# Feed-forward layers in two phases through DRAM, with seven block products in place of eight in 21 of 24 up-projection pairs

## The chip, the cores and the metric

The kernel runs on one core of a Trainium2 chip. The metric is the device time of one execution in microseconds (us), as the median of the runs shown. The engines are TensorE (PE in the rows; PEld is its weight load), VectorE (DVE), ScalarE (ACT), GpSimd (POOL) and SyncE (SP), which only issues transfers here.

## What is computed

A decoder of two layers on 1024 tokens with 1024 features, all in float32. Layer 0 mixes tokens with an RG-LRU, layer 1 with stick-breaking attention; behind each stands a gated feed-forward network, which is what the change touches:

```python
D_MODEL = 1024; SEQ = 1024; D_FF = 3 * D_MODEL; FFN_CONV = 3

def causal_depthwise_conv(x, w, b):
    K = w.shape[0]
    S = x.shape[1]
    xp = jnp.pad(x, ((0, 0), (K - 1, 0), (0, 0)))
    y = b + xp[:, 0:S] * w[0]
    for k in range(1, K):
        y = y + xp[:, k:k + S] * w[k]
    return y

def conv_ffn(x, w_up, conv_w, conv_b, w_down):
    h = causal_depthwise_conv(x @ w_up, conv_w, conv_b)
    return (jax.nn.gelu(h[..., :D_FF]) * h[..., D_FF:]) @ w_down

# per layer, with mix the RG-LRU (layer 0) or the attention (layer 1)
x = layer_norm(DN_ALPHA * x + mix, ln_g[layer, 0], ln_b[layer, 0])
f = conv_ffn(x, ffn_w_up[layer], ffn_conv_w[layer], ffn_conv_b[layer], ffn_w_down[layer])
x = layer_norm(DN_ALPHA * x + f, ln_g[layer, 1], ln_b[layer, 1])
```

## The kernel before

Float32 operands are held as a sum of two `fp32r` parts (`Split`: `hi`, a rounded copy, and `lo`, the rest). A product of two such operands is three matmuls: hi by hi, hi by lo, lo by hi. The residual stream `xres` is eight tiles of 128 tokens by 1024 features; its transpose `xT` (features by tokens, in two halves of 512 tokens) is made by `transpose_x`: PE transposes into PSUM, ACT casts the hi part (L219), DVE subtracts the lo part (L220).

Four stages follow each other: RG-LRU, feed-forward of layer 0, attention, feed-forward of layer 1. `ffn(layer, last)` goes over 24 pairs `j` of blocks of 128 hidden features, one gate block (`pg`) and one value block (`pu`). For each block `wblock` issues one load of 512 KB on SP's queue, a cast of the hi part on ACT (L83) and the subtraction of the lo part on POOL (L89). `project` makes 48 matmuls of 128x512 for a block (eight blocks of the contraction, two halves of the tokens, three matmuls each), so 96 for a pair. Pair 0 is done in quarters of 256 tokens (`project_quarter`, `mm3`) while the last tiles of the stage before are still being finished. `conv` does the convolution of width 3 from PSUM: an ACT Identity with scale and bias (L406) and two DVE multiply-adds (L408). Then come the gelu on ACT (L429), the product of gate and value on DVE (L431), and the split of the gated values on POOL (`mh` L87, `ml` L89), which stay in SBUF.

After every second pair `accumulate` adds the product of two earlier gated blocks and two blocks of `w_down` to `xres`: for each of eight token tiles 12 matmuls (L137, L138, L141) and two DVE additions (L149). The last four blocks go through `Finish`, tile by tile: the rest of the sum, the statistics on DVE (L162, L164), `rstd` on POOL (L166, L167), the normalisation (DVE L189, then ACT L192 and POOL L193, or DVE L196 for the last tiles), and what follows a tile: its transposes, or the store of the output.

The order on each engine is fixed when the program is built, by a scheduler that works from the tile pools (number of buffers per tag) and the order of the calls. An engine runs its instructions in that order; a wait at the head holds what stands behind it. All loads of weights stand in SP's queue in the same way.

## Time and profile before

| | before |
|---|---|
| median of 3 runs | 2514.78 us (2513.81 to 2517.9) |
| span of the profiled execution | 2509.8 us |
| PE busy | 2427.3 us, 97% of the span |
| DVE, POOL, ACT busy | 47%, 38%, 28% of the span |
| transfers | 125.71 MB, 50 GB/s over the span |
| first pair after the quarters, layer 0 and layer 1 | 369.2 us and 1733.8 us |
| last matmul of layer 0's and of layer 1's feed-forward | about 1139 us and 2496 us |

The profiled execution has no time of its own beside its span; the span is 5.0 us under the median of the runs. A busy engine in such a table is busy by the modelled ends of its instructions. A row of a timeline gives the start, the duration, the engine, the line, the operation with output and inputs, and in brackets how long the engine sat idle before it and what released it. A row of the groups by line gives count, sum and mean.

### The profile page before, as it was taken

The page shows a single profiled execution, that of the slowest core. Times are in us where ns is not written, and L with a number is a line of the kernel's source. Part 1 is how long each engine was busy: PE and PEld are TensorE (multiplying, and loading weights), DVE is VectorE, ACT ScalarE, POOL GpSimd, SP SyncE. Part 2 cuts the span into 40 slices and gives each one's busy share as a digit, 9 for nine tenths or more (in the row PEclk, how much of TensorE's full clock was granted, in tenths as well). Part 3 has the DMA queues.
Part 4 walks back from the last instruction along what each step waited for, and adds up shares of the span by engine and source line. Part 5 has one row for each costly group of instructions (what it writes and reads, how often), then busy time and mean ns, then how long its engine had stood idle before and what let it go on. Part 6 is the DMA issues. An engine that isn't in the chain of part 4 may idle for free.

```text
span 2509.8 us, 27143 instructions
## 1 busy us (share of the span) xinstructions
PE 2427.3 (97%) x11324; PEld 2008.6 (80%) x11324; DVE 1182.8 (47%) x1400; ACT 713.3 (28%) x951; POOL 953.0 (38%) x570
## 2 busy tenths in 40 slices
PE   8999889999999999999999999989999999999997
PEld 6877778888888888878877787768888888888886
DVE  5684852333333333364466555594433333333336
ACT  4644232212111122223433333343222122121221
POOL 4685354333333323353322222254533323333334
PEclk9999999999999999999999999999999999999999
DMA  6111112111111111210011101111211111111112
GB/s 216 47 53 51 42 34 60 50 51 51 46 47 51 51 50 43 68 42 26 28 32 34 29 31 34 35 33 43 76 43 51 48 45 51 45 48 51 51 34 84
DMA packets 36410, 125.71 MB, mean 50 GB/s; under 512 B 4032, under 2 KB 5696, under 8 KB 36288
## 3 DMA queue, kind: packets, MB, share of 16 engines
q1 hardware_dynamic: 31680, 110.11, 14.1%
q10 hardware_dynamic: 4608, 13.87, 1.7%
q8 instruction: 89, 1.46, 0.2%
q14 instruction: 33, 0.27, 0.0%
HBM read 119.78 MB, written 4.19 MB: 49 GB/s over the span
## 4 chain that ended last, share of the span: by engine, by line
PE 41%; DVE 5%; issue 5%; POOL 1%; ACT 1%; POOLq 0%; DVEq 0%; ACTq 0%
PE po L137 3%; PE pg L111 3%; PE pu L111 3%; PE pg L114 3%; PE pu L112 3%; PE pg L112 3%; PE po L141 3%; PE po L138 3%; PE pu L114 3%; PE pp L101 2%; PE pp L103 2%; PE pp L102 2%; DVE e L578 2%; DVE xres L549 1%; DVE b L579 1%
## 5 line engine op out<-in xcount | busy, mean ns | idle before, releaser
L89 POOL TENSOR_TENSOR wlo<-wraw,whi 128x1024 fp32r<-128x1024 f32 (+2 forms) x213 | 519.3, 2440 | 1082.8 <-ACT whi L83 1068.6
L83 ACT CAST whi<-wraw 128x1024 fp32r<-128x1024 f32 (+2 forms) x205 | 206.9, 1010 | 1139.5 <-PE pg L112 341.1
L137 PE MATMUL po<-whi,mh 128*128 128x512 f32 x896 | 353.1, 395 | 14.1 <-DVE xres L149 12.7
L138 PE MATMUL po<-wlo,mh 128*128 128x512 f32 x896 | 351.5, 392 | 0.0
L408 DVE SCALAR_TENSOR_TENSOR u<-pg,pv,u 128x1023 f32<-128x1023 f32 x96 | 123.1, 1282 | 436.9 <-ACT u L406 435.2
L149 DVE TENSOR_TENSOR xres<-xres,po 128x512 f32<-128x512 f32 x390 | 252.0, 681 | 162.6 <-PE po L141 160.3
L408 DVE SCALAR_TENSOR_TENSOR u<-pu,pv,u 128x1023 f32<-128x1023 f32 x96 | 123.0, 1281 | 392.3 <-ACT u L406 391.3
L112 PE MATMUL pg<-xTl,whi 128*128 128x512 f32 x736 | 286.3, 389 | 0.0
L111 PE MATMUL pg<-xTh,whi 128*128 128x512 f32 x736 | 286.3, 389 | 0.0
L111 PE MATMUL pu<-xTh,whi 128*128 128x512 f32 x736 | 286.3, 389 | 0.0
L112 PE MATMUL pu<-xTl,whi 128*128 128x512 f32 x736 | 286.3, 389 | 0.0
L141 PE MATMUL po<-whi,ml 128*128 128x512 f32 x896 | 280.6, 392 | 0.0
L114 PE MATMUL pg<-xTh,wlo 128*128 128x512 f32 x736 | 226.6, 389 | 0.0
L114 PE MATMUL pu<-xTh,wlo 128*128 128x512 f32 x736 | 226.6, 389 | 0.0
L137 PEld LDWEIGHTS po<-whi,mh 128*128 128x128 f32 x896 | 169.5, 189 | 56.6 <-DVE xres L149 16.4
L141 PEld LDWEIGHTS po<-whi,ml 128*128 128x128 f32 x896 | 169.3, 189 | 36.3
L138 PEld LDWEIGHTS po<-wlo,mh 128*128 128x128 f32 x896 | 169.7, 189 | 34.7
L101 PE MATMUL pp<-xTh,whi 128*128 128x512 f32 (+1 forms) x416 | 161.3, 388 | 0.0
L114 PEld LDWEIGHTS pg<-xTh,wlo 128*128 128x128 f32 x736 | 138.2, 188 | 28.7
L114 PEld LDWEIGHTS pu<-xTh,wlo 128*128 128x128 f32 x736 | 138.2, 188 | 28.7
L112 PEld LDWEIGHTS pu<-xTl,whi 128*128 128x128 f32 x736 | 138.2, 188 | 28.7
L111 PEld LDWEIGHTS pu<-xTh,whi 128*128 128x128 f32 x736 | 138.2, 188 | 28.6
(166 smaller groups left out, 3968.4 us busy)
## 6 DMA issues: line engine op xcount, KB each, us to landing
wraw<-in_w_up SPq DMA_DIRECT2D x96, 512.0 KB, 3.5
wraw<-in_w_down SPq DMA_DIRECT2D x48, 512.0 KB, 3.5
wraw<-in_w_in SPq DMA_DIRECT2D x14, 512.0 KB, 3.6
wraw<-in_w_o SPq DMA_DIRECT2D x9, 512.0 KB, 3.5
xres<-in_x ACTq DMA_DIRECT2D x8, 512.0 KB, 4.9
wraw<-in_w_out SPq DMA_DIRECT2D x8, 512.0 KB, 3.5
wraw<-in_w_q SPq DMA_DIRECT2D x8, 512.0 KB, 3.5
wraw<-in_w_k SPq DMA_DIRECT2D x8, 512.0 KB, 3.5
```

What stands on the lines that cost most here:

```text
L83: A.copy(out=hi, in_=src)
L89: eng.tensor_tensor(out=lo, in0=src, in1=hi.bitcast(F32), op=ALU.subtract)
L101: T.matmul(out, lhsT=l.hi, rhs=r.hi, start=start, stop=False)
L102: T.matmul(out, lhsT=l.hi, rhs=r.lo, start=False, stop=False)
L111: T.matmul(ps[h], lhsT=wc.hi, rhs=xT[h].hi[:, c, :], start=st, stop=False)
L112: T.matmul(ps[h], lhsT=wc.hi, rhs=xT[h].lo[:, c, :], start=False, stop=False)
L114: T.matmul(ps[h], lhsT=wc.lo, rhs=xT[h].hi[:, c, :], start=False, stop=sp)
L137: T.matmul(po[h], lhsT=g.hi, rhs=w.hi[:, d], start=st, stop=False)
L138: T.matmul(po[h], lhsT=g.hi, rhs=w.lo[:, d], start=False, stop=False)
L141: T.matmul(po[h], lhsT=g.lo, rhs=w.hi[:, d], start=False, stop=sp)
L149: V.tensor_tensor(out=xres[t][:, d], in0=xres[t][:, d], in1=po[h], op=ALU.add)
L408: V.scalar_tensor_tensor(out=u[:, k:], in0=ps[:, :S - k], scalar=cw[:, 2 - k:3 - k], in1=u[:, k:], op0=ALU.mult, op1=ALU.add)
```

## The change

Each feed-forward layer becomes two phases. `up` does all 24 pairs and stores each pair's gated values in float32 to DRAM (`gd[j]`, 512 KB on SP's queue). `down` loads them back in eight groups of three blocks with the three blocks of `w_down`, splits both (ACT cast, POOL subtraction), and accumulates each group over the eight token tiles with 18 matmuls per half. `Finish` takes the last six blocks, three of them added earlier to tiles 0 to 3.

In `up`, pairs 0, 1 and 23 are computed as before (`plain`), from weights in pieces of 128x512. The other 21 pairs of a layer go through `seven`. It views the pair as a product of 2 by 2 blocks: gate and value (rows), the two halves of the contraction (inner), the two halves of the tokens (columns), and forms it from seven products of blocks, of 12 matmuls each, in the Winograd form of Strassen's method. That needs four sums of weight blocks (`combine`, DVE), hi and lo parts for seven weight operands of 128x512, copies between PSUM banks (ACT, L551, L553, L559), two additions in PSUM (DVE, L556, L560), and four sums of the blocks of `xT`, which `sums_of_x` makes once per layer: 16 POOL subtractions of 128x512, 64 PE transposes, 16 ACT casts and 16 DVE subtractions.

```diff
+                ring = pool("ring", bufs=6)
+                uw = pool("uw", bufs=3)
+                rawp = pool("raw", bufs=6)
+                sums = pool("sums", bufs=4)
+                tq = pool("tq", bufs=1)
+                pcv = pool("pcv", bufs=2, space=PSUM)
+                pcg = pool("pcg", bufs=1, space=PSUM)
+                pp5 = pool("pp5", bufs=2, space=PSUM)
...
+                def operand(src):
+                    w = Split(ring.tile([P, HS], F32R, name="whi", tag="whi"),
+                              ring.tile([P, HS], F32R, name="wlo", tag="wlo"))
+                    split_sb(w.hi, w.lo, src)
+                    return w
+
+                def blocks(j):
+                    out = []
+                    for f in (j, NFF + j):
+                        for k in range(2):
+                            raw = rawp.tile([P, HS], F32, name="wraw", tag="wraw")
+                            nc.sync.dma_start(out=raw, in_=a["w_up"][layer, f][:, k * HS:(k + 1) * HS])
+                            out.append(raw)
+                    return out
...
+                def product(ps, w, x, start, stop):
+                    for c in range(4):
+                        wc = w[:, c * P:(c + 1) * P]
+                        for k, (l, r) in enumerate(((wc.hi, x.hi), (wc.hi, x.lo), (wc.lo, x.hi))):
+                            T.matmul(ps, lhsT=l, rhs=r[:, c, :], start=start and c == k == 0,
+                                     stop=stop and c == 3 and k == 2, skip_group_check=True)
...
                     V.tensor_tensor(out=ug, in0=ug, in1=uv, op=ALU.mult)
-                    ms = Split(gp.tile([P, S], F32R, name="mh", tag="mh"),
-                               gp.tile([P, S], F32R, name="ml", tag="ml"))
-                    split_sb(ms.hi, ms.lo, ug, hi_eng="pool", lo_eng="pool")
-                    gs.append(ms)
-                    if j % 2 == 1 and 3 <= j < NFF - 1:
-                        accumulate(psm, gs[j - 3:j - 1], down_weights(j - 3, 2), first=(j == 3))
+                    nc.sync.dma_start(out=gd[j], in_=ug)
+
+                def sums_of_x():
+                    for t in ((0, 1, 2, 3) if not last else (0, 1, 3, 2)):
+                        x, y = xres[t], xres[t + 4]
...
+                        for o, p, q in ((ts[0], y[:, lo_], x[:, lo_]), (ts[2], y[:, hi_], y[:, lo_]),
+                                        (ts[1], y[:, hi_], ts[0]), (ts[3], x[:, hi_], ts[1])):
+                            G.tensor_tensor(out=o, in0=p, in1=q, op=ALU.subtract)
+                        for i in (0, 2, 1, 3):
...
+                def seven(j):
+                    r11, r12, r21, r22 = blocks(j)
+                    (b11, b12), (b21, b22) = xq
+                    t1, t2, t3, t4 = Ts
+                    s1 = combine(ALU.add, r21, r22)
+                    s2 = combine(ALU.subtract, s1, r11)
+                    s3 = combine(ALU.subtract, r11, r21)
+                    s4 = combine(ALU.subtract, r12, s2)
+                    w11, w1, w2, w12, w3, w4, w22 = (operand(r) for r in (r11, s1, s2, r12, s3, s4, r22))
+                    cv = pcv.tile([P, S], F32, name="cv", tag="cv")
+                    c21, c22 = two(cv)
+                    p5 = pp5.tile([P, HS], F32, name="p5", tag="p5")
+                    product(c22, w11, b11, True, False)
+                    product(p5, w1, t1, True, True)
+                    cg = pcg.tile([P, S], F32, name="cg", tag="cg")
+                    c11, c12 = two(cg)
+                    A.copy(out=c11, in_=c22)
+                    p5s = uw.tile([P, HS], F32, name="p5s", tag="p5s", bufs=1)
+                    A.copy(out=p5s, in_=p5)
+                    product(c22, w2, t2, False, False)
+                    product(c11, w12, b21, False, True)
+                    V.tensor_tensor(out=c12, in0=c22, in1=p5s, op=ALU.add)
+                    product(c22, w3, t3, False, True)
+                    product(c12, w4, b22, False, True)
+                    A.copy(out=c21, in_=c22)
+                    V.tensor_tensor(out=c22, in0=c22, in1=p5s, op=ALU.add)
+                    product(c21, w22, t4, False, True)
+                    return cg, cv
...
+                NG = NFF // GROUP
+                for k in range(NG - 2):
+                    gs, ws = load(k)
+                    accumulate(pb, gs, ws, first=(k == 0))
...
+                gs, ws = load(NG - 2)
+                e = range(4)
+                accumulate(pb, gs, ws, False, tiles=e)
+                g2, w2 = load(NG - 1)
+                Finish(psm, gs + g2, ws + w2, gb, after, early=(GROUP, e), lag=0 if last else 4,
                        fast=2 if last else 0).run(range(NT))
```

In all the program has 9048 matmuls of 512 columns where there were 9552, the same 1008 of 256 columns, and 830 transposes where there were 702. ACT's instructions rise from 985 to 1413, DVE's from 1402 to 1560, POOL's from 575 to 781, and SP's from 222 to 414.

The seven products of a pair are called P1 to P7 below, in the order of the code. On PE the first four matmuls of the next pair's P1 stand ahead of a pair's P5.

**POOL at the start of the feed-forward of layer 0.** Before (`xres6`, `xres7` are the last two tiles of the RG-LRU stage; `wlo` of weight blocks stand among them):

```order
L89 TENSOR_TENSOR wlo_2556<-wraw_2553,whi_2555 128x1024
L193 TENSOR_TENSOR xres6_82<-xres6_82,lnb_1939 128x1024
L89 TENSOR_TENSOR wlo_2342<-wraw_2339,whi_2341 128x1024
L166 TENSOR_SCALAR rstd_2242<-mv_2240 128x1
L167 TENSOR_TENSOR rstd_2242<-rstd_2242,mhalf_74 128x1
L89 TENSOR_TENSOR wlo_2562<-wraw_2559,whi_2561 128x1024
L193 TENSOR_TENSOR xres7_83<-xres7_83,lnb_1939 128x1024
```

Now, behind the last L193 (`s` are sums of x; `wlo_2396` to `wlo_2408` belong to pair 0):

```order
L498 TENSOR_TENSOR s_2605<-xres4_79,xres0_75 128x512
L498 TENSOR_TENSOR s_2607<-xres4_79 128x512
L498 TENSOR_TENSOR s_2606<-xres4_79,s_2605 128x512
L498 TENSOR_TENSOR s_2608<-xres0_75,s_2606 128x512
L96 TENSOR_TENSOR wlo_2396<-wraw_2387,whi_2395 128x512
L96 TENSOR_TENSOR wlo_2400<-wraw_2389,whi_2399 128x512
L96 TENSOR_TENSOR wlo_2404<-wraw_2391,whi_2403 128x512
L96 TENSOR_TENSOR wlo_2408<-wraw_2393,whi_2407 128x512
```

The subtractions of `wlo` for pair 0 moved from between the last tiles to behind four subtractions of `sums_of_x` (six in layer 1).

**ACT in the middle of the layer.** Before, one pair (`u<-pg` and `u<-pu` are L406, `u<-u` the gelu):

```order
L83 CAST whi_4231<-wraw_4229 128x1024
L406 ACTIVATE u_3954<-pu_3840,pv_67 128x1024
L83 CAST whi_4237<-wraw_4235 128x1024
L406 ACTIVATE u_4073<-pg_3963,pv_67 128x1024
L429 ACTIVATE u_4073<-u_4073 128x1024
```

Now, the part of a pair from P5's end to the next pair's P3 (`cv_3085`, `cg_3111` are this pair's PSUM, `cv_3233`, `cg_3259` the next one's; the `whi` are the next pair's w12, w3, w4, w22):

```order
L90 CAST whi_3217<-wraw_3191 128x512
L559 COPY cv_3085<-cv_3085 128x512
L90 CAST whi_3221<-s_3201 128x512
L477 ACTIVATE u_3178<-cg_3111,pv_66 128x1024
L90 CAST whi_3225<-s_3203 128x512
L477 ACTIVATE u_3183<-cv_3085,pv_66 128x1024
L485 ACTIVATE u_3178<-u_3178 128x1024
L90 CAST whi_3229<-wraw_3195 128x512
L551 COPY cg_3259<-cv_3233 128x512
```

The copy that P3 of the next pair waits for came to stand behind this pair's gelu and a cast.

**DVE in the middle of the layer**, now, from one pair's last multiply-adds to the next pair's first (`s_3493` to `s_3497` are s1 to s3 of a pair two further on):

```order
L479 SCALAR_TENSOR_TENSOR u_3183<-cv_3085,pv_66,u_3183 128x1022
L487 TENSOR_TENSOR u_3178<-u_3178,u_3183 128x1024
L461 TENSOR_TENSOR s_3493<-wraw_3489,wraw_3491 128x512
L556 TENSOR_TENSOR cg_3259<-cv_3233,p5s_3261 128x512
L461 TENSOR_TENSOR s_3495<-s_3493,wraw_3485 128x512
L560 TENSOR_TENSOR cv_3233<-cv_3233,p5s_3261 128x512
L461 TENSOR_TENSOR s_3497<-wraw_3485,wraw_3489 128x512
L479 SCALAR_TENSOR_TENSOR u_3326<-cg_3259,pv_66,u_3326 128x1023
```

Sums of weights two pairs ahead came to stand in front of the additions in PSUM and of the multiply-adds. On SP the load of `wraw_3491` (r22) is issued when POOL has done the `wlo` of an earlier w11, and the store of gated values stands right behind it.

## Rows read from the trace of the kernel before

**Rows 1.** The page's part 1: busy time, share of the span and instructions.
```profile
PE 2427.3 (97%) x11324; PEld 2008.6 (80%) x11324; DVE 1182.8 (47%) x1400; ACT 713.3 (28%) x951; POOL 953.0 (38%) x570
```

**Rows 2.** Stretches: length, busy us of PE, PEld, DVE, ACT, POOL; granted clock, DMA.
```profile
345.00:355.00 10.00, 6.90 (x59) 6.70 (x58) 3.31 (x6) 2.26 (x5) 3.69 (x2) 1.00 0.20 60
500.00:1100.00 600.00, 600.00 (x2647) 496.24 (x2647) 212.21 (x245) 119.52 (x112) 201.75 (x95) 1.00 0.17 52
2500.00:2510.00 10.00, 0.00 (x0) 0.00 (x0) 5.57 (x8) 0.00 (x0) 1.83 (x2) 0.53 0.34 136
```

**Rows 3.** Timeline of PE, five places: start, duration, engine, line, operation.
```profile
369.22 0.40 PE L111 MATMUL pg<-xTh,whi 128*128 128x512 f32 x1
...
699.82 0.39 PE L137 MATMUL po<-whi,mh 128*128 128x512 f32 x1
...
701.18 0.39 PE L137 MATMUL po<-whi,mh 128*128 128x512 f32 x1
...
1733.78 0.40 PE L111 MATMUL pg<-xTh,whi 128*128 128x512 f32 x1
...
2495.77 0.39 PE L141 MATMUL po<-whi,ml 128*128 128x512 f32 x1
```

**Rows 4.** Timeline of PE at the end of RG-LRU: the last tile's transposes.
```profile
348.74 1.09 PE L214 MATMUL pt<-ident,xres 128*128 128x128 f32 x8 [3.10 <-POOL xres L193]
```

**Rows 5.** Groups by line and shape, ACT: count, busy us, mean ns, idle before.
```profile
L83 ACT CAST whi<-wraw 128x512 fp32r<-128x512 f32 x2 | 1.2, 620 | 0.8 <-DMA wraw<-in_w_in 0.8
L406 ACT ACTIVATE u<-pg,pv 128x1024 f32<-128x1024 f32 x48 | 57.5, 1198 | 9.7 <-PE pg L114 9.7
L429 ACT ACTIVATE u<-u 128x1024 f32<-128x1024 f32 x48 | 50.9, 1061 | 121.3 <-DVE u L408 121.3
L521 ACT COPY vt<-pp 128x512 f32<-128x512 f32 x16 | 9.3, 583 | 13.4 <-PE pp L103 13.4
```

**Rows 6.** Groups by line and shape, POOL and DVE.
```profile
L89 POOL TENSOR_TENSOR wlo<-wraw,whi 128x1024 fp32r<-128x1024 f32 x199 | 502.3, 2526 | 1057.8 <-ACT whi L83 1043.8 <-DVE whi L85 8.4 <-DVE th L331 4.3
L89 POOL TENSOR_TENSOR wlo<-wraw,whi 128x512 fp32r<-128x512 f32 x2 | 2.6, 1292 | 11.3 <-ACT whi L83 11.2
L408 DVE SCALAR_TENSOR_TENSOR u<-pg,pv,u 128x1023 f32<-128x1023 f32 x48 | 61.6, 1283 | 435.2 <-ACT u L406 435.2
L149 DVE TENSOR_TENSOR xres<-xres,po 128x512 f32<-128x512 f32 x390 | 252.0, 681 | 162.6 <-PE po L141 160.3
L431 DVE TENSOR_TENSOR u<-u 128x1024 f32<-128x1024 f32 x48 | 59.2, 1234 | 0.9
L89 DVE TENSOR_TENSOR xTl<-xraw,xTh 128x512 fp32r<-128x512 f32 x8 | 5.4, 687 | 3.4 <-ACT xTh L83 3.4
L189 DVE SCALAR_TENSOR_TENSOR xres<-xres,mv,lng 128x1024 f32<-128x1024 f32 x32 | 57.5, 1798 | 0.3
```

**Rows 7.** Timeline of POOL and DVE where L189 meets a subtraction, and alone.
```profile
339.88 2.39 POOL L89 TENSOR_TENSOR wlo<-wraw,whi 128x1024 fp32r<-128x1024 f32 x1
...
340.54 2.82 DVE L189 SCALAR_TENSOR_TENSOR xres<-xres,mv,lng 128x1024 f32<-128x1024 f32 x1
...
2493.36 1.28 DVE L189 SCALAR_TENSOR_TENSOR xres<-xres,mv,lng 128x1024 f32<-128x1024 f32 x1
```

**Rows 8.** Timeline at the end: POOL's last long addition, DVE's last addition.
```profile
2496.31 2.34 POOL L193 TENSOR_TENSOR xres<-xres,lnb 128x1024 f32<-128x1024 f32 x1 [1.26 <-ACT xres L192]
...
2500.79 0.68 DVE L149 TENSOR_TENSOR xres<-xres,po 128x512 f32<-128x512 f32 x1
```

**Rows 9.** Timeline of POOL: the last L193 ahead of each feed-forward layer.
```profile
346.34 2.35 POOL L193 TENSOR_TENSOR xres<-xres,lnb 128x1024 f32<-128x1024 f32 x1
...
1712.76 2.35 POOL L193 TENSOR_TENSOR xres<-xres,lnb 128x1024 f32<-128x1024 f32 x1 [1.26 <-ACT xres L192]
```

**Rows 10.** Transfers: target and source, queue, count, KB each, median us to landing.
```profile
wraw<-in_w_gates SPq DMA_DIRECT2D x8, 128.0 KB, 2.6
...
wraw<-in_w_in ACTq DMA_DIRECT2D x2, 256.0 KB, 3.3
```

157 lines of the change are left out of this document (112 added, 45 removed).

## Prediction

> **What bounds the kernel now.** I read the busy times first. PE is busy 97% of the span, DVE 47%, POOL 38%, ACT 28% [rows 1]. Then the stretches, to see whether PE has any hole where the change works: from 500 to 1100 us, inside the feed-forward of layer 0, it is busy 600.00 of 600 us at a granted clock of 1.00, the level of 2.4 GHz [rows 2], with POOL and DVE at a third of the time. Then the timeline: six 128x512 matmuls start within 701.18 − 699.82 = 1.36 us, 0.2267 us each [rows 3] (the 0.39 us of a row overlap). Layer 1 reads the same: from 1733.78 to 2495.77 us there are 762 us [rows 3], and 3360 matmuls (23 pairs of 96 and 24 blocks of 48) at 0.2267 us are 761.7 us. So both layers are a solid row of matmuls, no engine but PE counts there, and each matmul removed is worth its 0.2267 us as long as the row stays solid. What the change can lose is that solidity.
>
> **The change part by part.** Sums are made against the profiled span, 2509.8 us; the median of the runs is 5.0 us above it, which I add at the end.
>
> *Removed.* A pair of seven products has 84 matmuls instead of 96. Two layers times 21 pairs times 12 are 504, the count that the program also shows: 504 × 0.2267 = **−114.3**. The down-projection keeps its count (18 per half and tile for three blocks, as 12 for two).
>
> *Added on PE.* 128 transposes for the sums of x. The last tile's eight took 1.09 us with the pipeline's end of about 0.15 [rows 4], so 0.13 each: **+16.9**.
>
> *Start of the up phase.* Before, pair 0's weights were split by POOL between the last tiles of the stage ahead; now behind the last L193 and four subtractions of x (six in layer 1). A 128x512 subtraction is 1.29 us alone and 1.26 as half of the 1024 wide one [rows 6]; I take 1.25 in a row. Layer 0: the last L193 ended at 348.7 [rows 9]. Some 2.4 us of POOL's weight work ahead of it [rows 7] is gone, so it ends near 346.3; four subtractions bring 351.3, pair 0's four `wlo` 356.3. PE can only do its first quarters at that pace; the last needs 12 matmuls of 256 columns (0.12 each, the half of 0.24), then six of eight quarter-blocks of 24 remain: 356.3 + 1.4 + 17.3 = 375.0, against 369.22 [rows 3]: +5.8. Layer 1: L193 near 1712 instead of 1715.1 [rows 9], six subtractions, one `wlo`, one more subtraction, three `wlo`, 11 × 1.25 = 13.8, then 18.7 as before: 1744.5 against 1733.78 [rows 3], +10.7. About ten of the transposes fall into these waits (−1.5). Sum **+15**, between 8 (POOL is done earlier, as the L193 of tiles ahead also move up) and 26 (a wait for space for the weights on top). Here PE is thinned, not stopped; a stretch in which it did 6.90 of 10 us still had a clock of 1.00, while one without any work had 0.53, near the level of 1.2 GHz [rows 2].
>
> *Sums of x beside pair 1.* Twelve subtractions, 15 us of POOL, then six `wlo` for pair 2, 7.5 us: 22.5 against pair 1's 96 × 0.2267 = 21.8. With releases between, 2 per layer: **+4** (0 to 12).
>
> *The steady pair.* 84 matmuls are 19.04 us. Per pair POOL has seven subtractions, 8.8 us; ACT seven casts, three copies, two Identities and a gelu, about 9 (casts in a row start 0.53 apart by estimate, 0.62 alone); DVE four sums at 0.69, two additions at 0.68, four multiply-adds at 1.28, a product at 1.23: 10.5 [rows 5, 6]. None is near 19, so only chains through these engines to a PE wait cost something. There are two.
>
> Chain A goes from P6's end to the next pair's P3, which overwrites the bank that the copy L551 reads. P6's result is out 0.21 us after its last start pitch; ACT casts w3 (0.53), POOL subtracts (0.08 + 1.29) and frees the sum's buffer, DVE forms the s3 that stands ahead of the multiply-adds (0.05 + 0.69); the Identity (1.20) runs beside that. Then two multiply-adds 2.57, gelu 1.06 + 0.05, cast of w22 0.53, copy 0.59, 0.05 to PE: 7.7 us [rows 5, 6]. PE has P7 and the next pair's P1 and P2 to cover it, 32 matmuls (four of P1 ran earlier): 7.25 us. Stall 0.43, with a restart of 0.11 **0.54 us a pair**. The copy is from PSUM to PSUM, which no row shows; I take L521's 0.58 [rows 5], from PSUM to SBUF. From below nothing (a copy of half that length gives 0.25), from above L406's 1.20 for twice the width (+0.6).
>
> Chain B goes to P5, which waits for the addition L556, queued on DVE behind the next but one pair's s1. s1 waits for POOL's `wlo` of w1 (P3's end + 0.21 + 0.53 + 0.08 + 1.29 + 0.05), then 0.69 + 0.68 + 0.05: 3.58 against P4 and four matmuls, 3.63. It also waits for the load of r22, issued when POOL has done w11's `wlo`, about 6.8 us into the pair (P2's end 4.5, behind w22's `wlo` to 5.5, then 1.25). A 256 KB load on SP's queue isn't in the trace; 128 KB takes 2.6 and 256 KB on ACT's queue 3.3 [rows 10]: I take 2.9. Landing 9.7, addition done 11.1; P5 is due at 10.9 plus chain A's 0.4, 11.3. Nothing, with 0.2 us to spare.
>
> 42 × 0.54 = **+23**, from 0 to 50.
>
> *Store and reload of the gated values.* Per pair 512 KB written, 3 MB read per group of 144 matmuls (32.6 us, 96 GB/s; layer 0 now runs at 52 [rows 2]). A group's six blocks are 6 × 2.4 = 14.4 us on POOL [rows 6], hidden by the 32.6 of the group before. At the seam pair 23 (21.8 us of matmuls) hides the first group, ready some 18 us after its last values: **+2** for both layers (0 to 6). Without that cover a seam would cost the 18 us. At layer 0's end the next weights come about 3 us later and the tiles, now 8.2 us apart, no longer wait for DVE: 0 (±3).
>
> *The end.* Before, DVE's last addition was at 2500.79 though PE's last matmul started at 2495.77 [rows 3, 8]: DVE had stood behind a POOL result, which stood behind L193 from 2496.31 [rows 8]. A tile now has 36 matmuls, 8.2 us, so that L193 is done before: **−4** (−5 to −2).
>
> **Sum.** −114.3 + 16.9 + 15 + 4 + 23 + 2 − 4 = −57.4: span 2452.4, run **2457 us**.
>
> A row speaks against this change more than the sum shows. L189 alone takes 1.28 us; the one issued at 340.54 took 2.82 and ended 1.1 after POOL's subtraction that ran until 342.27 [rows 7], and its mean is 1.80, while L408 and L149 with one operand in PSUM never move from 1.28 and 0.68 [rows 6]. So a DVE operation on two SBUF inputs waits out a POOL operation. The Trainium skill states it in "SBUF — State Buffer", section "SBUF: two separate sides": a DVE instruction with two SBUF inputs and a GpSimd one that reads SBUF share a port pair as an exclusive lock, and whoever starts first keeps it for the whole instruction. The trace agrees. The new sums and the product are of that kind. In the steady pair s3 starts when POOL has just ended w3's `wlo`, and its next one waits for a cast that P7 holds back; s1 likewise. Only the product (about 5.8 into the pair) meets w11's `wlo` (5.5 to 6.8); it loses 1 us, and nobody waits for it but the store. The sum holds if this order holds.
>
> **Rivals.** (1) *The product goes first.* If it takes the port 0.3 us before w11's `wlo`, that waits up to 1.23, r22's load is issued as much later, and with 0.2 to spare chain B stalls P5 about 1.1 us more: 42 × 1.15 = +48, **2505**. A load that lands in 3.6 because the store of 512 KB runs beside it does part of the same. For it: 0.3 us decide. Against: ACT's copy and cast sit ahead of w11's subtraction only by estimate. (2) *Slower than before.* The lock falls on both chains: s3 waits out a subtraction on A (+1.25), s1 on B (+1.25 less 0.2 to spare), and the product case comes on top, some 2.25 more a pair: +95, **2552**. It decides from where the stalls reach 81/42 = 1.9 us a pair (the sum without the 23), four times my figure. For it: L189's mean, 0.5 over its undisturbed time. Against: POOL is busy 8.8 of 19 us, and at both places its next instruction waits for PE. (3) *The row stays solid.* The copy is quick, no stall, and POOL reaches pair 0's weights at once: −23, −7 at the starts, −4 beside pair 1: **2423**. For it: chain A is over its cover by only 6%.
>
> **How the numbers follow.** Forecast 60%, rival 1 17%, rival 3 14%, rival 2 9%. The range takes rivals 1 and 3 in with a little for the transitions, 2420 to 2510; above it lies rival 2. A measurement of this kernel tells 0.2% (5 us) from no change. Faster by more: 0.87 (forecast, rival 3 and most of rival 1); within 0.2%: 0.04 (rival 1 and 2 halfway); slower: 0.09.
>
> **What would show it.** PE's count of 128x512 matmuls down by 504 at the same 0.2267 us. Waits of PE for ACT's copy L551 (42 times, about 0.4) and few for DVE's L556; if L556 leads with over 1 us, rival 1; both over 1 us, rival 2. At the starts PE waits for POOL's `wlo`, pair 1 beginning some 6 and 11 us later in its layer. In the down phase and at the seams hardly any wait. Wrong would be a pitch other than 0.2267 in the products, waits for the reload in every group, or a granted clock under 1.00 in the up phases.

## The result, and the profile after

The changed kernel took 2474.23 us (2469.55 to 2475.37, 4 runs) against 2514.3 us (2511.46 to 2517.9, 4 runs) of the kernel before on the same chip: a ratio of 0.9837, 95% interval 0.9823 to 0.9851. It is faster, and the time lies inside the range, 17 us above the forecast. The span fell from 2509.8 to 2473.7 us, by 36.1 where the sum said 57.4, so 21.3 us of the expected gain are missing in the traces. By the medians it is 40.1 and 17.3: the profiled execution of after is the slowest of its four (2475.37 us), and that of before, 2509.8 us of span and the 1.7 by which a run's time exceeds its span, was 2.8 under its median.

The head of the page of after (columns as in [rows 1]):

```profile
span 2473.7 us, 28596 instructions
PE 2369.8 (96%) x10948; PEld 1935.4 (78%) x10948; DVE 1331.9 (54%) x1558; ACT 926.5 (37%) x1379; POOL 1126.3 (46%) x776
PEclk9999989999999999999999999998999999999999
```

PE lost 57.5 us of busy time against [rows 1], yet its share fell by a point: the row of matmuls has holes now. The list of PE's waits says where (columns: engine, line, its tile, what it waited for, us in total, times, the longest). The lines on L469, L479 and L135 touch the change:

```profile
PE cv L469 <- DVE cg L556: 9.3, 9, 2.1
PE po L153 <- DVE u L479: 8.1, 2, 4.0
...
PE pg L135 <- POOL wlo L96: 4.0, 2, 2.5
PE pp L135 <- POOL wlo L96: 2.5, 1, 2.5
...
PE cv L469 <- ACT cg L551: 0.3, 1, 0.3
```

L556 is the addition that P5 waits for (chain B, priced at nothing), L479 at L153 is the seam from the up to the down phase, L135 is pair 0 (`pg`) and the start of attention (`pp`). L551, the copy at the end of chain A, shows once. A line counts idle time behind the modelled end of the matmul before, and with 0.39 us of duration at starts 0.2267 apart this end lies 0.16 past the next due start. Gaps of less than about 0.3 us therefore get no line; they show between two starts.

I cut the span at the same places as the sum. Of a layer's 64 transposes I count 16 to the stretch ahead of pair 1 and 48 to the one behind it, a division that the prediction doesn't make. The measured column is worked out from starts of matmuls in both traces.

| stretch | predicted | measured |
|---|---|---|
| start to pair 1, layer 0 (369.22 to 377.23) | +7.2 | +8.0 |
| pair 1 to last down-projection matmul, layer 0 (770.0 to 746.4 us) | −36.3 | −23.6 |
| from there to pair 1, layer 1 (594.5 to 609.9) | +12 | +15.3 |
| pair 1 to last matmul, layer 1 (762.0 to 731.5) | −36.3 | −30.5 |
| behind the last matmul (14.0 to 8.7) | −4 | −5.3 |

So the transitions cost some 3 us more, and 18.5 of the 21.3 us lie in the two feed-forward layers themselves, 12.7 of them in layer 0.

**The pairs.** With 84 matmuls a pair is 19.04 us. Between the first and the last of a layer's 21 seven-product pairs lie 20 intervals; they took 404.9 us in layer 0 and 393.2 in layer 1 (20.24 and 19.66 each), 24.1 and 12.4 over. In starts of matmuls: the gaps ahead of P5 sum to 11.45 us in layer 0 and 2.85 in layer 1, those ahead of P3 to 3.85 and 4.12, and each of these 78 stops (a layer's first pair has none ahead of P3) is followed by a second gap of 0.10 to 0.11, 9 us in all, and by 0.03 more at the start after that. Behind two of the stops PE runs at the lower clock for a while, some 3 us in all. Summed by place, the stops at P5 take 23.1 and those at P3 13.4 of the 36.5 us. Three P5 gaps are 2.29 us long, all in layer 0. DVE around one of them, and then POOL (start, duration, engine, line, operation; in brackets the idle time before and what ended it):

```profile
720.05 1.59 DVE L461 TENSOR_TENSOR s<-wraw 128x512 f32<-128x512 f32 x1 [3.34 <-DMA wraw<-in_w_up]
721.57 0.69 DVE L556 TENSOR_TENSOR cg<-cv,p5s 128x512 f32<-128x512 f32 x1
```

```profile
717.12 1.29 POOL L96 TENSOR_TENSOR wlo<-s,whi 128x512 fp32r<-128x512 f32 x1 [1.49 <-ACT whi L90]
719.83 1.26 POOL L96 TENSOR_TENSOR wlo<-s,whi 128x512 fp32r<-128x512 f32 x1 [1.43 <-DMA gd<-u]
```

then SP, whose first row is the load of r22, and the matmul that waited:

```profile
715.66 0.33 SPq L455 DMA_DIRECT2D wraw<-in_w_up  x1
```

```profile
719.79 0.39 PE L469 MATMUL cv<-xTh,whi 128*128 128x512 f32 x1
722.31 0.50 PE L469 MATMUL cv<-Th,whi 128*128 128x512 f32 x1 [2.13 <-DVE cg L556]
722.65 0.40 PE L469 MATMUL cv<-Tl,whi 128*128 128x512 f32 x1
```

Against this, a pair in which it went as the sum had it:

```profile
440.98 0.69 DVE L461 TENSOR_TENSOR s<-wraw 128x512 f32<-128x512 f32 x1 [1.91 <-DMA wraw<-in_w_up]
441.69 0.70 DVE L556 TENSOR_TENSOR cg<-cv,p5s 128x512 f32<-128x512 f32 x1
```

```profile
439.49 1.29 POOL L96 TENSOR_TENSOR wlo<-s,whi 128x512 fp32r<-128x512 f32 x1 [1.50 <-ACT whi L90]
442.22 1.29 POOL L96 TENSOR_TENSOR wlo<-s,whi 128x512 fp32r<-128x512 f32 x1 [1.43 <-DMA gd<-u]
```

Read the bracket of L461, the s1 two pairs ahead: it waited for a load. In the good pair r22's load was issued at 438.02 and s1 started 2.96 later (the forecast had 2.9), a good 1.2 ahead of POOL's next subtraction. In the bad pair it was issued at 715.66 and s1 started 4.39 later, 0.22 behind a subtraction of POOL's, and then needed 1.59 instead of 0.69. L556 stands behind s1, and P5 behind L556. A load that lands over 1.2 us late so falls into POOL's operation and pays for that too. All three long gaps come out at 2.29, because in each s1 ends 0.55 behind POOL's operation, whenever in it the load landed.

The other gaps follow the landing too. In all 40 intervals r22's load is issued 4.3 to 4.4 us before P5 is due, and the gap is what the landing takes beyond 2.9 us, to within 0.1 (landing 3.17, gap 0.24; landing 3.86, gap 0.97), but never under 0.05; past 4 us of landing it jumps to 2.29. The median of the 40 landings is 3.04 us (2.57 to 4.64), so there was nothing to spare.

What the late landings have in common stands in the DMA records. While the bad pair's load was under way (715.66 to 719.93) one packet of 16 KB ran on the queue whose kind is called instruction:

```profile
q8 instruction: 1, 0.02, 2.3%
```

Such a packet meets r22's load in 7 of the 20 intervals of layer 0, and these are its seven longest gaps, 0.40 us and over, 9.9 of the 11.45 us. In layer 1 none of the 20 loads meets one, and its longest gap is 0.49. The trace of e2 below parts in the same way (seven gaps of 0.52 and over with such a packet, 0.44 at most without). Packets on the other queue of that kind, q14, don't go with late landings: r22's load met 16 KB of them once and landed after 2.94. That is a coincidence in time, read from traces; no run moved these packets.

**The seam.** PE at the start of layer 0's down phase, and DVE ahead of it:

```profile
858.02 0.47 PE L153 MATMUL po<-dh,mh 128*128 128x512 f32 x1 [4.03 <-DVE u L479]
858.33 0.44 PE L154 MATMUL po<-dl,mh 128*128 128x512 f32 x1
858.56 0.63 PE L153 MATMUL po<-dh,mh 128*128 128x512 f32 x1
858.99 0.63 PE L154 MATMUL po<-dl,mh 128*128 128x512 f32 x1
...
862.44 0.40 PE L153 MATMUL po<-dh,mh 128*128 128x512 f32 x1
```

```profile
855.27 2.60 DVE L479 SCALAR_TENSOR_TENSOR u<-pu,pv,u 128x1023 f32<-128x1023 f32 x2 [3.74 <-ACT u L477]
```

```profile
848.16 2.39 POOL L96 TENSOR_TENSOR dl<-draw,dh 128x1024 fp32r<-128x1024 f32 x1
```

The first blocks of the down phase were split by 850.55, 7.5 us early, so the reload was hidden as forecast. What PE waited for is space in PSUM: the multiply-adds of pair 23 that read `pu` end at 857.87, and the first product is written to those banks. Then 8 matmuls start 0.427 apart instead of 0.2267 (granted clock 0.61 from 858.0 to 862.4). Layer 1 has the same wait (4.02).

**The start of layer 0.** PE at pair 0, and the stretches around it (columns: window, length, busy time of PE, PEld, DVE, ACT and POOL with their instructions, granted clock, DMA share, GB/s):

```profile
347.65 0.58 PE L135 MATMUL pg<-xTh,whi 128*128 128x256 f32 x1 [1.24 <-ACT whi L90]
...
351.58 0.58 PE L135 MATMUL pg<-xTh,wlo 128*128 128x256 f32 x1 [2.49 <-POOL wlo L96]
351.96 0.41 PE L135 MATMUL pg<-xTh,whi 128*128 128x256 f32 x1
...
357.80 0.28 PE L135 MATMUL pu<-xTl,whi 128*128 128x256 f32 x1
357.92 0.28 PE L135 MATMUL pu<-xTh,wlo 128*128 128x256 f32 x1
```

```profile
340.00:350.00 10.00, 4.80 (x29) 3.41 (x28) 6.47 (x10) 7.39 (x13) 7.67 (x7) 0.83 0.16 52
350.00:360.00 10.00, 8.42 (x51) 8.42 (x52) 0.00 (x0) 0.20 (x1) 7.70 (x7) 0.66 0.52 157
360.00:370.00 10.00, 10.00 (x85) 10.00 (x85) 0.00 (x0) 0.32 (x1) 0.00 (x0) 1.00 0.01 4
```

From 340 to 350 us PE was busy 4.80 of 10 us; it waited 2.49 up to 351.58, and then two dozen matmuls of 256 columns ran 0.21 apart, until 356.5, where later ones take 0.12.

### The profile page after: what moved, and what is told of

Its sections match the earlier page's. It is cut to its first block, busy times and chain, and to the rows that moved or that the text cites. A ratio compares the mean times of both kernels' runs of the same rounds, so it can differ in the third digit from the quotient of the medians.

```text
span 2473.7 us, 28596 instructions
## 1 busy us (share of the span) xinstructions
PE 2369.8 (96%) x10948; PEld 1935.4 (78%) x10948; DVE 1331.9 (54%) x1558; ACT 926.5 (37%) x1379; POOL 1126.3 (46%) x776
## 4 chain that ended last, share of the span: by engine, by line
PE 74%; DVE 11%; issue 7%; POOL 3%; DMA 3%; ACT 2%; DVEq 0%; POOLq 0%; SPq 0%; ACTq 0%
PE cv L469 18%; PE cg L469 8%; PE po L153 8%; PE po L154 8%; PE po L157 8%; PE p L469 4%; PE pp L114 2%; PE pp L115 2%; PE pp L116 2%; DVE e L747 2%; DMA wraw<-in_w_up 2%; DVE xres L718 1%; PE pg L135 1%; POOL wlo L96 1%; DVE b L748 1%
## 5 line engine op out<-in xcount | busy, mean ns | idle before, releaser
L96 POOL TENSOR_TENSOR wlo<-wraw,whi 128x512 fp32r<-128x512 f32 (+2 forms) x219 | 365.7, 1680 | 451.7 <-ACT whi L90 436.7
L96 POOL TENSOR_TENSOR wlo<-s,whi 128x512 fp32r<-128x512 f32 x168 | 218.4, 1300 | 247.2 <-ACT whi L90 212.9
L153 PE MATMUL po<-dh,mh 128*128 128x512 f32 x768 | 301.2, 392 | 8.1 <-DVE u L479 8.1
L154 PE MATMUL po<-dl,mh 128*128 128x512 f32 x768 | 300.5, 391 | 0.0
L90 ACT CAST whi<-wraw 128x512 fp32r<-128x512 f32 (+2 forms) x211 | 146.8, 700 | 305.9 <-PE cv L469 149.5
L157 PE MATMUL po<-dh,ml 128*128 128x512 f32 x768 | 238.8, 391 | 0.0
L469 PE MATMUL cv<-Th,whi 128*128 128x512 f32 x504 | 206.7, 410 | 11.6 <-DVE cg L556 9.3
L469 PE MATMUL cv<-Tl,whi 128*128 128x512 f32 x504 | 198.2, 393 | 0.0
L469 PE MATMUL cv<-Th,wlo 128*128 128x512 f32 x504 | 197.9, 393 | 0.0
L153 PEld LDWEIGHTS po<-dh,mh 128*128 128x128 f32 x768 | 145.1, 189 | 39.5 <-ACT dh L90 8.8
L461 DVE TENSOR_TENSOR s<-wraw 128x512 f32<-128x512 f32 x84 | 61.8, 735 | 206.6 <-POOL wlo L96 122.6
L154 PEld LDWEIGHTS po<-dl,mh 128*128 128x128 f32 x768 | 145.3, 189 | 30.0
L469 PEld LDWEIGHTS cv<-Th,whi 128*128 128x128 f32 x504 | 95.3, 189 | 60.4 <-DVE cg L556 24.7
L469 PE MATMUL cg<-xTl,whi 128*128 128x512 f32 x336 | 130.7, 389 | 0.0
```

The source lines that it names most:

```text
L90: A.copy(out=hi, in_=src)
L96: eng.tensor_tensor(out=lo, in0=src, in1=hi.bitcast(F32), op=ALU.subtract)
L153: T.matmul(po[h], lhsT=g.hi, rhs=w.hi[:, d], start=st, stop=False)
L154: T.matmul(po[h], lhsT=g.hi, rhs=w.lo[:, d], start=False, stop=False)
L157: T.matmul(po[h], lhsT=g.lo, rhs=w.hi[:, d], start=False, stop=sp)
L461: V.tensor_tensor(out=s, in0=x, in1=y, op=op)
```

## The experiments

All times beside are medians of four executions; the ratio is to the kernel before, with its 95% interval. "After" is the changed kernel, 2474.2 us. Stretches quoted as four numbers are the 20 intervals of layer 0, of layer 1, from the last interval to the down phase of layer 0, and the down phase of layer 0: after has 404.9, 393.2, 43.2, 265.4.

**e1_plain: the two phases without the seven products.** It tells what store, reload and seams cost by themselves.

```diff
-        PLAIN = (0, 1, NFF - 1)
+        PLAIN = range(NFF)
...
-                    if j == 0:
-                        sums_of_x()
```

> All 24 pairs of both layers by eight products, in the two phases of the changed kernel, without sums of x: the phases alone. The 504 matmuls come back (+114.3 us), 128 transposes go (-17), the waits and restarts inside the pairs go (-34 by the gaps between matmuls in the changed kernel's trace), the x sums ahead of and beside the first pairs go (-10 to -17). Theory (the products are worth some 50 us net, the phases cost a few): 2474 + 50 = 2524 us, 4 to 14 us slower than before, with the two seams still waiting 4 us each. Rival (the phases are what eats the gain, by reloads that hold PE in each group): 2540 us or more. Rival (the phases are free and all losses are in the seven products): 2510 us, not slower than before.

2529.2 us, 1.0059 (1.0044 to 1.0074). The two phases alone cost some 15 us, and the seven products bring 55 (2529.2 − 2474.2) where their terms in the sum, −114.3 + 16.9 + 23 + 4 and a part of the starts, made about 60. Its waits name the seam just as after's do:

```profile
PE po L153 <- DVE u L479: 8.0, 2, 4.0
```

So the seam belongs to the two phases and not to the products. For the phases alone the sum has +2 at the seams, −4 at the end and, by estimate, 5 of the 15 at the starts, 3 in all: here 12 of the 17 us lie that are missing by the medians.

The trace of e1 shows more of the starts than that estimate. Without any sums of x pair 1 still begins 5.3 us later than before in layer 0 (with them 8.0), and the stretch to pair 1 of layer 1 is 13.9 longer (with them 15.3). The first matmul of pair 0 in layer 0, before and in e1:

```profile
338.63 0.36 PE L101 MATMUL pg<-xTh,whi 128*128 128x256 f32 x1
```

```profile
348.28 0.58 PE L135 MATMUL pg<-xTh,whi 128*128 128x256 f32 x1 [1.24 <-ACT whi L90]
```

Before, 29 of pair 0's 192 matmuls ran ahead of the last tile's transposes; in the two phases all stand behind them. Of the 13.9 us in layer 1's stretch 3.5 arise at the start of attention, whose first product waits for a `wlo` (2.5 us, the line on `pp` L135 in the list above).

**e2_seam: other PSUM for the first tiles of the down phase.** Its first two tiles go to banks of their own pools, which pair 23 doesn't use for `pu`; all later ones go to `psm`.

```diff
-                pb = pool("pb", bufs=4, space=PSUM)
                 psm = pool("ps", bufs=4, space=PSUM)
+                p45 = pool("p45", bufs=2, space=PSUM)
+                p67 = pool("p67", bufs=2, space=PSUM)
...
-                    accumulate(pb, gs, ws, first=(k == 0))
+                    if k == 0:
+                        accumulate(p67, gs, ws, True, tiles=(0,))
+                        accumulate(p45, gs, ws, True, tiles=(1,))
+                        accumulate(psm, gs, ws, True, tiles=range(2, NT))
+                    else:
+                        accumulate(psm, gs, ws, False)
...
-                accumulate(pb, gs, ws, False, tiles=e)
+                accumulate(psm, gs, ws, False, tiles=e)
```

> The first two token tiles of a layer's down phase use the PSUM banks that P5 and the gate half left, the others the four banks that free last. Theory (at the seam PE waits for the PSUM of pair 23, held until its last multiply-add, 4.1 us, and then runs 8 to 10 matmuls at half the clock, 2.3 us): both seams lose most of it, -9 to -13 us, run near 2463. Rival (the first group's reload and split are as late as the multiply-adds, as the prediction's 18 us had it): the wait stays and is named after POOL or a transfer, change under 2 us.

2462.6 us, 0.9791 (0.9777 to 0.9806): 11.6 less. The wait for L479 is gone from the list, and the stretch to the down phase fell from 43.2 to 39.0 in both layers, the down phase of layer 0 from 265.4 to 263.6. That is PSUM shown as the cause: loads and splits are the same. But the stretch from there to layer 1's first pair grew by 5.2 (641.7 to 646.9), and the pairs of layer 0 lost 4.2 of their excess, for no reason in the edit that I know of; the gaps at P5 differ from after's, as they do in e4. e9 below has a better split of the banks.

**e3_raw7: one more buffer for the raw weights.** The load of r22 then waits for an older buffer and is issued earlier; nothing else changes.

```diff
-                rawp = pool("raw", bufs=6)
+                rawp = pool("raw", bufs=7)
```

> One more buffer for the raw weight blocks (7 for 6), so that the load of r22 is issued when the subtraction of an earlier block ends, 1.3 us sooner or more. Theory (P5 waits for the landing of r22 through s1 and the addition behind it, and a landing 0.6 us later than usual lets POOL's next subtraction take the port first): the waits at P5, 14.3 us in 40 pairs of the changed kernel, fall under 5, those over 1 us are gone, run -12 to -18, near 2459. Rival (s1 is held by the subtraction of w1, the load only ends a little later): waits at P5 fall by less than a third, run -2 to -5.

2455.7 us, 0.9767 (0.9751 to 0.9783): 18.5 less. The gaps ahead of P5 fell from 11.45 and 2.85 to 1.03 and 0.99 us, the intervals to 391.0 and 391.3, and L556 left the list of PE's waits, in which the seam and the copy stay as they were. L556 itself now waits for P4's product 41 times (in after 8 times):

```profile
DVE cg L556 <- PE cg L469: 20.8, 41, 4.5
...
PE po L153 <- DVE u L479: 8.0, 2, 4.0
...
PE cv L469 <- ACT cg L551: 0.3, 1, 0.3
```

The gaps ahead of P3 stayed (3.82 and 4.09). So 15.7 of the 23.1 us at P5 ran through the late load of r22, as the second sentence of rival 1 had it. The other 7.5, a gap of 0.05 with its restart in each pair, stay, behind P4's own product. The orders leave no other cause: on PE and POOL the order is the same in both kernels, and on DVE and ACT it differs only in a few rows at the first pairs of the second layer.

**e4_sums_on_dve: the sums of x on DVE.**

```diff
-                            G.tensor_tensor(out=o, in0=p, in1=q, op=ALU.subtract)
+                            V.tensor_tensor(out=o, in0=p, in1=q, op=ALU.subtract)
```

> The 16 subtractions of x a layer on VectorE instead of GpSimd. Theory (POOL's four to six subtractions ahead of pair 0's weights set the start of the up phase): the first wlo comes 5 us sooner in layer 0 and 7 in layer 1, and PE's stretch at half the clock there is shorter: run -9 to -14, near 2463. Rival (the transposes and casts behind the last tile set the start): -4 or less. Rival (VectorE's subtractions wait for POOL's at the shared port and PE waits for the sums' transposes instead): no change, with waits of the x-sum transposes for DVE.

2463.8 us, 0.9801 (0.9787 to 0.9816): 10.4 less. The first seven-product pair of layer 0 starts at 405.1 instead of 410.0, that of layer 1 2.5 earlier against the end of layer 0. Of these 7.4 us about 4 lie ahead of pair 1 (3.6 in layer 0, 0.4 in layer 1), where POOL's subtractions stood ahead of pair 0's `wlo`, and the other 3.5 beside pair 1, where POOL did the rest of the subtractions. The first `wlo` comes 3.6 us sooner in layer 0 and 2.9 in layer 1, where 5 and 7 were expected. The rest, −8.5 in the pairs of layer 0 and +4.1 in those of layer 1, I put down to where late loads happen to fall, as the edit touches no pair; e7 bears that out.

**e5_sums3: three buffers for the sums of weights instead of four.** This changes the order on DVE. Four buffers put s1 (two pairs on) ahead of L556, and s3 ahead of the multiply-adds; three put s4 ahead of L556, s1 behind it, and s2 ahead of the multiply-adds.

```diff
-                sums = pool("sums", bufs=4)
+                sums = pool("sums", bufs=3)
```

> Three buffers for the sums of weight blocks instead of four, raw blocks as in the changed kernel: on VectorE s1 of the pair after next now stands behind the addition L556, and s4 stands ahead of it, which waits for no load that is late. Theory (the load of r22 reached P5 only because s1 stood ahead of L556): waits at P5 fall as with the seventh raw buffer, from 14.3 us to 2 or 3, run near 2457. Rival (the seventh buffer helped by something else, for instance by loads that come sooner for the casts): P5 keeps most of its waits, run 2468 to 2474.

2450.3 us, 0.9749 (0.973 to 0.9769): 24.0 less, and 7 less than I had expected. DVE, as above:

```profile
512.21 0.69 DVE L461 TENSOR_TENSOR s<-wraw,s 128x512 f32<-128x512 f32 x1 [1.75 <-POOL wlo L96]
513.07 0.70 DVE L556 TENSOR_TENSOR cg<-cv,p5s 128x512 f32<-128x512 f32 x1 [0.17 <-PE cg L469]
```

L556 now waits for its own product and for no load: gaps ahead of P5 1.02 and 0.97, ahead of P3 2.77 and 2.74 (0.15 each instead of 0.2), intervals 390.0 and 389.9. Chain B is thus cut a second time, by order and not by an earlier load. The 7 us that I had not expected are at the starts: 2.8 ahead of layer 0's first such pair and 4.3 in the stretch to layer 1's. Three buffers also changed the order on POOL, where pair 0's `wlo` now stand ahead of the last subtraction of x for the first tiles. PE's wait for them is 1.15 instead of 2.49:

```profile
349.50 0.58 PE L135 MATMUL pg<-xTh,wlo 128*128 128x256 f32 x1 [1.15 <-POOL wlo L96]
```

That is 1.3 of the 2.8 of layer 0, and 0.7 were there before (the last normalised tile came that much earlier); the rest and the 4.3 of layer 1 I have not traced.

**e6_raw7_sums5: seven raw buffers, five for sums, five for the low parts.** It was to cut chain A as well.

```diff
-                rawp = pool("raw", bufs=6)
-                sums = pool("sums", bufs=4)
+                rawp = pool("raw", bufs=7)
+                sums = pool("sums", bufs=5)
...
-                              ring.tile([P, HS], F32R, name="wlo", tag="wlo"))
+                              ring.tile([P, HS], F32R, name="wlo", tag="wlo", bufs=5))
```

> Seven raw buffers and five for the sums (five instead of six for the lo parts, to make room): s3 no longer stands directly ahead of the multiply-adds behind a subtraction. Theory (P3 waits 0.2 us and restarts 0.1 us late in each pair because the chain of w3's subtraction, s3, multiply-adds, gelu, cast and copy is longer than its cover): that chain gets some 0.6 us shorter and the wait goes: 42 x 0.3 = 12.6 us under the run with seven raw buffers, near 2443. Rival (the copy is held by ScalarE's own queue, cast and Identity of the same pair, not by s3): P3's gap stays at 0.2, run 2454 to 2457. Rival (five lo buffers hold POOL): new waits for wlo, slower than 2456.

2475.6 us, 0.9849 (0.9833 to 0.9864): 20 more than e3, where I had expected 13 less. The gaps ahead of P3 are gone. From P6's last start to the end of the copy L551 it takes 7.12 us (median) where after and e3 have 7.63, and the multiply-adds start 0.87 sooner, so chain A did run through the s3 that stood ahead of them. In their place (the first line is POOL's, and e3 has no such line):

```profile
POOL wlo L96 <- PE cv L469: 254.7, 159, 2.8
...
PE cv L469 <- DVE cv L560: 7.5, 37, 0.5
...
PE pg L135 <- POOL wlo L96: 6.5, 2, 3.7
```

L560 is the addition that P7 waits for. DVE, POOL and PE at one of the 37:

```profile
520.93 0.69 DVE L461 TENSOR_TENSOR s<-s,wraw 128x512 f32<-128x512 f32 x1 [0.75 <-POOL wlo L96]
524.82 0.69 DVE L461 TENSOR_TENSOR s<-wraw 128x512 f32<-128x512 f32 x1 [3.20 <-POOL wlo L96]
525.43 0.69 DVE L560 TENSOR_TENSOR cv<-cv,p5s 128x512 f32<-128x512 f32 x1
```

```profile
523.50 1.29 POOL L96 TENSOR_TENSOR wlo<-s,whi 128x512 fp32r<-128x512 f32 x1 [2.60 <-PE cv L469]
```

```profile
526.18 0.50 PE L469 MATMUL cv<-Th,whi 128*128 128x512 f32 x1 [0.20 <-DVE cv L560]
```

With a fifth buffer the scheduler moved s3 up to stand ahead of L560; it waits there for POOL, POOL for PE, and P7 starts 0.36 late in each pair. That POOL waits for PE comes with the five buffers for the low parts: a buffer is free again only when the product that read it is done, where in e3 POOL waits for ACT's casts. That is the third line of the expectation, new waits through five `lo` buffers, and e6 changes both counts at once, so it doesn't tell which of the two made the loss. 11 of the 20 us lie in the pairs, 5.6 in the stretch to layer 1; the latter I have not traced.

**e7_raw7_seam_dve: e3, e2 and e4 together.**

```diff
-                rawp = pool("raw", bufs=6)
+                rawp = pool("raw", bufs=7)
...
-                            G.tensor_tensor(out=o, in0=p, in1=q, op=ALU.subtract)
+                            V.tensor_tensor(out=o, in0=p, in1=q, op=ALU.subtract)
...
+                        accumulate(p67, gs, ws, True, tiles=(0,))
...
```

> Seven raw buffers, the seam's banks and the sums of x on VectorE together. If the three causes are separate the gains add, 18.5 + 11.6 + 10.4 = 40.5 us: 2434. If they share waits (the clock's slow stretches, or a stage that absorbs another's gain) 2440 to 2448.

2444.7 us, 0.9724 (0.9707 to 0.974). The three gains alone sum to 40.5, together they are 29.6: what e2 and e4 won in the pairs of layer 0 was a part of chain B's excess, which the raw buffer removes already (intervals 391.2 and 391.4, as in e3), and the loss behind e2's seam is in it too (643.6 to layer 1's first such pair, 4.5 over e4).

**e8_raw7_sums5_seam_dve: the same with e6's buffers**, five for sums and for the low parts.

```diff
-                rawp = pool("raw", bufs=6)
-                sums = pool("sums", bufs=4)
+                rawp = pool("raw", bufs=7)
+                sums = pool("sums", bufs=5)
...
-                            G.tensor_tensor(out=o, in0=p, in1=q, op=ALU.subtract)
+                            V.tensor_tensor(out=o, in0=p, in1=q, op=ALU.subtract)
...
```

> The same with five sum buffers. If chain A's wait goes: 2421. If five lo buffers or ScalarE's queue hold it: 2434 or more.

2458.8 us, 0.9781 (0.9765 to 0.9796): 14 more than e7, intervals 401.4 and 395.8. e6's loss comes with the buffers (both counts) and not with what is around them.

**e9_sums3_seam: e5 with another split of PSUM at the seam.** Only the first two tiles go to `psm`, all later ones to `pb`.

```diff
-                sums = pool("sums", bufs=4)
+                sums = pool("sums", bufs=3)
...
-                    accumulate(pb, gs, ws, first=(k == 0))
+                    if k == 0:
+                        accumulate(psm, gs, ws, True, tiles=(0, 1))
+                        accumulate(pb, gs, ws, True, tiles=range(2, NT))
+                    else:
+                        accumulate(pb, gs, ws, False)
```

> Three sum buffers, and at the seam the first two token tiles use the four PSUM banks that the gate half and P5 left, all other tiles the banks of the changed kernel. In the first seam run the wait went but the stretch from layer 0's end to layer 1's first pair grew by 5 us, since its final tiles used the banks that attention takes first. Theory (that is what gave part of the gain back): the seams give 13 to 15 us, that stretch stays at some 637 us, run near 2436. Rival (the 5 us came from attention's own state and not from the banks): 2440 or more.

2439.2 us, 0.9706 (0.9692 to 0.9721). The stretch to the down phase is 39.0 (e5: 43.2), the down phase of layer 0 263.6 (265.3), that of layer 1 260.9 (262.5): 5.9 and 5.8 a layer, which is what the seam cost in after. The stretch to layer 1's first pair stays at 638.9 (e5: 637.4), so e2's loss there came from its banks.

**e10_sums3_seam_dve: e9 with the sums of x on DVE.**

```diff
-                sums = pool("sums", bufs=4)
+                sums = pool("sums", bufs=3)
...
-                            G.tensor_tensor(out=o, in0=p, in1=q, op=ALU.subtract)
+                            V.tensor_tensor(out=o, in0=p, in1=q, op=ALU.subtract)
...
+                        accumulate(psm, gs, ws, True, tiles=(0, 1))
...
```

> The same with the sums of x on VectorE. Theory (POOL's subtractions ahead of pair 0's weights cost the start of each layer): 5 us in layer 0 and up to 5 in layer 1, near 2427. Rival (with three sum buffers the subtractions of x no longer stand ahead of pair 0's weights, so that there is nothing left to win): 2434 to 2437.

2436.0 us, 0.9695 (0.9681 to 0.971). 3 us less than e9, within what the two intervals allow for; the first seven-product pair starts at 407.6 (e9: 407.3). With three sum buffers, which have let pair 0's weights past one of these subtractions already, DVE has nothing left to win there.

**e11_sums3_raw7_seam_dve: e10 with seven raw buffers.** On top of e10:

```diff
-                rawp = pool("raw", bufs=6)
+                rawp = pool("raw", bufs=7)
```

> The same with a seventh raw buffer. With s1 behind the addition L556 the load of r22 has 2 us or more to spare, so a buffer more should change nothing beyond 2 us, if the raw buffers helped only through r22. If the loads held something else as well, up to 5 us less.

2437.2 us, 0.9697 (0.9681 to 0.9713): no difference to e10, intervals 389.9 and 389.8. Once s1 stands behind L556, an earlier load brings nothing; both edits cut the same chain.

e10 beats both kernels: 38 us under the changed one and 3.05% under the one before. e9 and e11 can't be told from it.

## Why the prediction was right, and where it was short

**Right: what bounds the kernel and what a matmul is worth.** 504 matmuls of 512 columns are gone, and those left start 0.2267 us apart wherever nothing is waited for. The reload is hidden in every group, the product L487 loses to the port lock as said (2005 ns a piece in after against 1234 of L431 in [rows 6]) and nobody waits for it:

```profile
L487 DVE TENSOR_TENSOR u<-u 128x1024 f32<-128x1024 f32 x48 | 96.3, 2005 | 4.5
L551 ACT COPY cg<-cv 128x512 f32<-128x512 f32 x42 | 24.3, 579 | 0.0
```

Also right: the copy from PSUM to PSUM (579 ns for 0.58 taken) and nearly the landing of a 256 KB load on SP's queue (2.9 taken, 3.04 the median of r22's).

**Chain A, +23: the mechanism right, the size over.** The stall ahead of P3 is 0.20, its restart 0.11 and 0.03 behind that, 0.34 a pair where I had 0.54. Over the 40 intervals that is 13. From P6's end to the end of the copy the chain takes 7.40 us where the sum had 7.65; 0.19 of the difference lies ahead of the multiply-adds and 0.12 in the cast of w22. e6 shows that it runs through s3. In e5 s2 stands in the place of s3, and the gap shrinks only to 0.15.

**Chain B, "nothing, with 0.2 us to spare": the step that failed most.** It cost 14.3 us of gaps and 9 behind them, restarts and 3 us of lower clock, 23 in all. What failed is the spare of 0.2 us: a landing of 2.9, the one that the sum took, leaves nothing to spare, half of the landings are above 3.04, and what is above 2.9 costs its full length. The landing isn't one number. From issue to s1 it was 2.96 in one pair and 4.39 in another, and of 40 gaps ahead of P5 22 stayed at 0.12 or under, while three reached 2.29. The second effect is in the price: past 1.2 us late, s1 meets POOL's operation and waits that out as well, a lock that I had placed at the product alone. That is the lock on s1 of rival 2, in three pairs and not in all. Rival 1 named the late landing, at 0.7 and in every pair; it was spread instead, and large in a few. The late landings fall together with packets of instructions, and only in layer 0 do these meet r22's load; that they cause them is not shown, since the cutting of the chain was tried, not the traffic. And 7.5 of the 23 us are a path that the sum didn't have: L556 waits for P4's own product as well, and the four matmuls ahead of P5 cover its addition but for 0.05 us. The granted clock under 1.00 in an up phase, which the forecast named as a sign of being wrong, came behind two of the long stops (0.55 from 421.3 to 425.1).

**The seam, +2 for both layers: the wrong wait was priced.** The forecast asked when the reload is ready, and that was right by 7.5 us. It didn't ask whose PSUM the first product takes. It takes pair 23's, which is free after its last multiply-adds: 4.0 us of wait and slow matmuls behind it. e9 puts it at 5.9 and 5.8, so +11.7 for both, 9.7 over. e1 shows it without the seven products, e2 and e9 without the wait.

**The starts, +15: the number right, its reason only in part.** +8.0 and +15.3 were measured for 7.2 and 12, 4.1 over; 3.5 of this arise at the start of attention and belong to another term, below. The step counted POOL's subtractions of x; without them the same steps give pair 1 some 1 us late in layer 0 and 2 in layer 1, but e1, which has none, is 5.3 and 13.9 late (10.4 without attention's part). So it missed what the two phases do by themselves, and took the subtractions at more than they cost; that the two made up for each other is luck. It also let six quarter-blocks of pair 0 remain behind POOL's last `wlo`, and in the trace of layer 0 seven remain. "PE is thinned, not stopped" was wrong: the granted clock was 0.83 and 0.66 from 340 to 360 us, and two dozen matmuls of 256 columns at 0.21 instead of 0.12 cost 2.2 us. The 0.53 of [rows 2] was the row to take.

**Beside pair 1, +4 for both layers: about right.** +2.0 and +0.9 were measured. **The tail, −4:** −5.3, just past its bound of −5. **The end of layer 0, 0 (±3): inside its bounds, −1.8.** Attention starts 3.5 us late behind its weights, for about 3. Before, layer 0 took 770.0 us where its 3360 matmuls need 761.7, so it was no solid row to its end: transposes and two waits for DVE (2.05 and 1.47 us) stood among the last tiles. In after those waits are gone and 2.9 of the 8.3 us are left, 5.3 less.

Together: chain B 23.1 over, the seams 9.7, the last pair of each layer (behind the 40 intervals) 1.9 in all, the starts 0.6; chain A 9.6 under, the end of layer 0 1.8, the tail 1.3, beside pair 1 1.1. That makes 21.5 where 21.3 are missing.

**What cancelled.** With chain A, the end of layer 0, the tail and the time beside pair 1 at their measured sizes the forecast would have stood 14 us lower, 31 from the result. Terms that were too high hid part of those that were too low, and that the result lies within 17 us is so far luck. The chances, most of which lay on "faster", rest on the first step, what a matmul is worth, and this held. The lowest time of rival 3, 2423, is 13 us under what e10 reaches with both waits cut: even then a pair needs 19.50 us, and of the 0.46 over 19.04 some 0.15 + 0.11 is at P3 and 0.05 + 0.11 at P5, with 0.03 behind each. Whether this can be had is open.

## What to carry to other kernels

A chain with 0.2 us to spare isn't free if a DMA stands in it: price it by how far its landing spreads (here 2.57 to 4.64 us), and first see whether the waiting instruction can stand ahead of what waits for the load. Where one stage follows another, ask of each resource that the first instruction needs when it was last read, PSUM banks as well as data. Buffer counts set the order of work too: here one sum buffer fewer brought 24 us, and one more, together with a ring of five low parts in place of six, cost 20 us.
